# Three of the sixteen double units of a first channel-mix product, made in seven products

## The chip, the cores and the metric

The kernel runs on one core of a Trainium2 chip. The metric is device time in microseconds, the median of several executions. A core has five engines that run side by side, each through its own queue of instructions: TensorE (PE; its weight loads appear as PEld), VectorE (DVE), ScalarE (ACT), GpSimd (POOL) and SyncE (SP). Transfers between main memory and the core's own memory (SBUF) are issued from the queues of SP, ACT and POOL. TensorE writes its results to eight banks of PSUM, from which VectorE and ScalarE evict them.

## The reference, cut to what matters

Two layers (DEPTH = 2) act on x of 512 frames by 1024 features. Each has a mixing part (mLSTM and retention branches with gates), then a channel mix, then a per-layer embedding:

```python
h2 = rmsnorm(x, norm2_g[i])
x = x + jnp.square(jax.nn.relu(h2 @ w_ff1[i] + b_ff1[i])) @ w_ff2[i] + b_ff2[i]
```

`w_ff1` is 1024 by 4096 and `w_ff2` 4096 by 1024. The change concerns the first of these two products, `h2 @ w_ff1`. After it come the per-layer embedding of the layer and, after the second layer, a final norm.

## The kernel before, in words

**Layout and precision.** Activations are kept transposed, features on the 128 partitions and the 512 frames along the free dimension, so x is eight tiles of 128 by 512. Every product is made in split precision: each operand is held as a high part (`wh`, `n2h`, ...; rounded by ScalarE at line 287) and a low part (`wl`, `n2l`, ...; the remainder, by VectorE at line 288), and each product is three matmuls: high by high, high by low, low by high (lines 451 to 453 for whole units, 501 to 503 for units in seven products).

**Whole units.** `t8` (line 442 and on) makes 128 output features: eight input tiles times three matmuls, 24 matmuls over 512 columns into one PSUM bank. Its weights, 128 by 1024 values, come from the array `wstream` with one transfer on SP, and are converted once by ScalarE and once by VectorE.

**Units in seven products.** `run_pair` makes 256 output features at once. The weight block and the activation are cut in two by two quarters, and seven products of quarters or of sums of quarters give the result in place of eight (the scheme of Strassen and Winograd). Each product is 12 matmuls over 256 columns. The order is P1, P5, P6, P2, P3, P7, and the last one, P4, is put off (`later`) until the next unit has made its first 12 matmuls (`flush`). Three PSUM banks serve: P6, P7 and P4 go where P1 was, P3 where P5 was, so each must wait until the earlier one is evicted. Weights come as pieces: A (block B11 and sum t1), C (B22 and t3), B (B21 and the sum t2, formed by VectorE at line 433), D (t4, formed at line 430). t1 and t3 are formed ahead in main memory by transfers on POOL's queue (`step`, line 336: a copy and an adding copy each), in the order of `groups()`, paced by a credit that the matmuls feed. The activation also needs four sums of quarters. For the gates and projections of the mixing part those sums are made once a layer by `xs_sums` through `operand_sums`, and `sevenfold` hands the right quarter to each product; `pair_tiles` evicts the seven products into two 512-column tiles, P1, P5, P6 and P4 by ScalarE and P2, P3 and P7 by VectorE.

**The channel mix.** The 4096 hidden features are four groups of 1024; each group is four double units of 256 (so there are sixteen in a layer), made by `ff1(b, p)` from two whole units. The second product is made group by group in seven products (`ff2`, tiles named o). The order is `ff_order`: f00 to f03, f10, then o00 to o03, f11 to f13, f20, o10 to o13, f21 to f23, f30, o20 to o23, f31 to f33; then, with a half of the embedding product between, o30 to o33. `ff1` evicts each unit by a multiplication with the norm's factor (line 1395, VectorE), Relu and square (lines 1396 and 1397, ScalarE) into a staging buffer `st` (two of them), then forms quarters and sums as operands of the second product (`pair_quarters`, `pair_operand`). The factor of the norm is not known when f00 starts; `n2.finish` and `n2.spread` make it during f00.

**What sets the order.** Weights are loaded and converted ahead in the order of the list of units: `ready` keeps conversion two places ahead for whole units and as `READY` says for pieces; there are three pairs of buffers for converted weights and four for raw ones. The order on each engine is otherwise made by a scheduler that places instructions by priority, which is their place in the program, when their operands and buffers are there.

Of the kernel before, what the change touches and what calls it, by code (L numbers as in the profile page):

```python
# [35 lines left out]
F32 = mybir.dt.float32  # L36
# [6 lines left out]
P = 128  # L43
T = 512
# [34 lines left out]
def ff_order():  # L79

    seq = [("f", 0, p) for p in range(4)]
    for b in range(3):
# [4 lines left out]

PRODUCTS = {"P1": ("A", 0, 0), "P5": ("A", 1, 4), "P2": ("B", 0, 2), "P6": ("B", 1, 5), "P3": ("C", 0, 6),  # L90
            "P7": ("C", 1, 3), "P4": ("D", 0, 1)}

# [35 lines left out]
def groups():  # L128


    g = {}
    for i in range(L):
        def rqk(h):
            return [("w_in", 0, c + k * 256) for k in (h, h + 1) for c in (CRQ, CRK)]

        def rg(h):
            return [("w_in", 0, CRG + h * 512 + 256 * p) for p in range(4)]

        g[i, "rv0"] = [("w_in", 0, CRV)]
        g[i, "rqk0"] = rqk(0)  # L140
        g[i, "gm"] = [("w_in", 0, CGM + 256 * p) for p in (2, 3)]
        g[i, "rg0"] = rg(0)
        g[i, "rv2"] = [("w_in", 0, CRV + 1024)]
        g[i, "rqk2"] = rqk(2)
        g[i, "rg2"] = rg(2)
        g[i, "gr"] = [("w_in", 0, CGR + 256 * p) for p in range(4)]
        for b in range(4):
            g[i, f"ff{b}"] = [("w_ff2", b * 1024, 256 * p) for p in range(4)]
    return g


def unit_list(i):

    u = [("IF",)]

    def t8(w, col, row=0):
        u.append(("T8", w, row, col))

    def v(col):
        for k in range(4):  # L160
            u.append(("V", k, col))

    def pair(g, p):
        u.append(("PAIR", (i, g), p))

    def mqk(h):
        for d in range(2):
            t8("w_in", CQ + h * 256 + d * P)
        for d in range(2):
            t8("w_in", CK + h * 256 + d * P)  # L170

    def mo(h):
        for d in range(2):
            t8("w_in", CO + h * 256 + d * P)

    def rqk(h):
        for a in range(2):
            pair(f"rqk{h // 2 * 2}", h % 2 * 2 + a)

    def rg(h):  # L180
        for a in range(2):
            pair(f"rg{h // 2 * 2}", h % 2 * 2 + a)

    def full(w, col=0, row=0, lo=0, hi=8):
        for c in range(lo, hi):
            t8(w, col + c * P, row)

    mqk(0)
    v(CV)
    full("w_in", CGM, 0, 0, 2)  # L190
    mqk(1)
    mo(0)
    full("w_in", CGM, 0, 2, 3)
    mqk(2)
    mo(1)
    v(CV + 512)
    mqk(3)
    mo(2)
    full("w_in", CGM, 0, 3, 4)
    mo(3)  # L200
    u.append(("WIDE", (i, "rv0"), 0))
    full("w_bm", 0, 0, 0, 4)
    rqk(0)
    for p in (2, 3):
        pair("gm", p - 2)
        full("w_bm", 0, 0, 2 * p, 2 * p + 2)
    rqk(1)
    rg(0)
    u.append(("WIDE", (i, "rv2"), 0))
    rqk(2)  # L210
    rg(1)
    rqk(3)
    full("w_br")
    rg(2)
    rg(3)
    for p in range(4):
        pair("gr", p)
        full("w_br", 0, 1024, 2 * p, 2 * p + 2)
    full("w_out")

    def pairs(seq):
        for kind, b, p in seq:
            if kind == "f":
                t8("w_ff1", b * 1024 + 256 * p)
                t8("w_ff1", b * 1024 + 256 * p + P)
            else:
                pair(f"ff{b}", p)

    pairs(ff_order()[0])
    u.append(("PE", 0))  # L230
    pairs(ff_order()[1])
    u.append(("PE", 1))
    full("w_pe_gate")
    return u


def build(ctx, tc, ins, out):
# [8 lines left out]
    def phase(name, side, bufs=1):  # L246
        return tc.alloc_tile_pool(name=name, bufs=bufs, side=side, reuse_waits="tile")
# [478 lines left out]
    def bcol(i, n, k):  # L726
        o, _ = _B[n]
        return bc[:, i, o + k:o + k + 1]
# [210 lines left out]
    for i in range(L):  # L939
# [443 lines left out]
        shift(cur["ff"], ph_side, True)  # L1383
        cur["ntmp"] = 2
        hid = {}

        def ff1(b, p):

            nm = f"l{i}f{b}{p}"
            hid[b, p] = [cur["ff"].tile([P, 7 * S], F32R, name=f"l{i}h{a}{b}{p}", tag=f"h{a}", bufs=5) for a in "hl"]  # L1390
            st = cur["ff"].tile([P, 8 * S], F32, name=nm + "st", tag="st", bufs=2)

            def evac(d, o):
                a = st[:, d * T:(d + 1) * T]
                ve.tensor_tensor(a, o, n2.b, OP.mult)
                ac.activation(a, a, AF.Relu, bias=bcol(i, "bf1", 8 * b + 2 * p + d))
                ac.activation(a, a, AF.Square)

            o = t8(n2.act, f"{nm}0")
            if b == 0 and p == 0:  # L1400
                n2.finish()
                o1 = t8(n2.act, f"{nm}1")
                n2.spread()
                evac(0, o)
                evac(1, o1)
            else:
                evac(0, o)
                evac(1, t8(n2.act, f"{nm}1"))
            pair_quarters(st, *hid[b, p])
            pair_operand(nm, st, *hid[b, p])  # L1410
# [39 lines left out]
        for kind, b, p in first:  # L1450
# [3 lines left out]
            if (b, p) == (3, 1):  # L1454
                pth, ptl = [cur["ff"].tile([P, 2, T], F32R, name=f"l{i}pt{a}", tag=f"h{a}", bufs=5) for a in "hl"]
                for k in range(2):
                    t = tmp(f"l{i}ptr{k}")
                    nc.scalar.dma_start(t, ins["pT"][i, k])
                    split(t, pth[:, k, :], ptl[:, k, :])
            ff1(b, p)  # L1460
        n2_pool.release()
        n3_pool = phase(f"n3{i}", act_side)
        n3 = Norm(f"l{i}n3", i, "g3", acts(n3_pool, f"l{i}n3"))
# [235 lines left out]
```

## Time and profile before

| | |
|---|---|
| median of 3 runs | 2336.89 us (2335.52 to 2338.47) |
| the profiled execution | 2338.24 us, span 2336.5 us |
| PE busy | 2317.7 us, 99% |
| DVE busy | 1722.3 us, 74% |
| ACT busy | 1224.1 us, 52% |
| POOL busy | 401.4 us, 17% |
| moved by DMA | 394.95 MB, mean 169 GB/s |

The span is the stretch from the first to the last instruction of one profiled execution; the time of that execution holds a little around it. Busy times are sums over an engine's instructions. Matmuls overlap in TensorE's pipeline, so the time from one matmul's start to the next tells more than the length of one. Layers are named l0 and l1; in the first layer the channel mix's first product runs from 772.6 us to about 1068 us.

### The profile page before, as it was taken

The page shows a single profiled execution, that of the slowest core. Times are in us where ns is not written, and L with a number is a line of the kernel's source. Part 1 is how long each engine was busy: PE and PEld are TensorE (multiplying, and loading weights), DVE is VectorE, ACT ScalarE, POOL GpSimd, SP SyncE. Part 2 cuts the span into 40 slices and gives each one's busy share as a digit, 9 for nine tenths or more (in the row PEclk, how much of TensorE's full clock was granted, in tenths as well). Part 3 has the DMA queues.
Part 4 walks back from the last instruction along what each step waited for, and adds up shares of the span by engine and source line. Part 5 has one row for each costly group of instructions (what it writes and reads, how often), then busy time and mean ns, then how long its engine had stood idle before and what let it go on. Part 6 is the DMA issues. An engine that isn't in the chain of part 4 may idle for free.

```text
span 2336.5 us, 35728 instructions
## 1 busy us (share of the span) xinstructions
PE 2317.7 (99%) x13664; PEld 2055.3 (88%) x13664; DVE 1722.3 (74%) x2658; ACT 1224.1 (52%) x1771; POOL 401.4 (17%) x618
## 2 busy tenths in 40 slices
PE   9999999999999999999999999999999999999998
PEld 8888898898998898899888888998989988998997
DVE  7878767896665577678778777778957656776785
ACT  6756544554554445445557564454636445445464
POOL 3122212112114212112422221000000020000012
PEclk9999999999999999999999999999999999999999
DMA  6665886668688777777766666434443442333431
GB/s 214 166 172 155 249 230 183 195 176 224 176 239 253 197 205 191 206 203 189 212 177 172 154 178 196 145 121 151 129 138 114 157 154 99 127 109 94 136 122 55
DMA packets 150540, 394.95 MB, mean 169 GB/s; under 512 B 19344, under 2 KB 22800, under 8 KB 150368
## 3 DMA queue, kind: packets, MB, share of 16 engines
q1 hardware_dynamic: 99808, 247.50, 32.6%
q0 software_dynamic: 35152, 117.73, 22.9%
q10 hardware_dynamic: 15408, 27.43, 3.5%
q8 instruction: 107, 1.75, 0.3%
q14 instruction: 65, 0.53, 0.1%
HBM read 373.71 MB, written 123.73 MB: 213 GB/s over the span
## 4 chain that ended last, share of the span: by engine, by line
PE 84%; issue 6%; DVE 5%; DMA 2%; ACT 2%; POOL 1%; SPq 0%; ACTq 0%; DVEq 0%; POOLq 0%
PE l1f L451 2%; PE l0f L451 2%; PE l0f L452 2%; PE l1f L452 2%; PE l1f L453 2%; PE l0f L453 2%; PE l1br L451 1%; PE l0br L451 1%; PE l0br L453 1%; PE l1br L452 1%; PE l0br L452 1%; PE l1br L453 1%; PE l0pg L451 1%; PE l0pg L453 1%; PE l1bm L451 1%
## 5 line engine op out<-in xcount | busy, mean ns | idle before, releaser
L287 ACT ACTIVATE wh<-wr 128x1024 fp32r<-128x1024 f32 (+1 forms) x223 | 231.2, 1044 | 286.4 <-issue 62.9
L288 DVE TENSOR_TENSOR wl<-wr,wh 128x1024 fp32r<-128x1024 f32 (+1 forms) x221 | 272.4, 1234 | 73.7 <-ACT wh L287 73.5
L287 ACT ACTIVATE wh_B<-wr 128x1024 fp32r<-128x1024 f32 x100 | 105.9, 1059 | 149.8 <-PE l1bm L452 13.1
L288 DVE TENSOR_TENSOR wl_B<-wr,wh_B 128x1024 fp32r<-128x1024 f32 x100 | 122.0, 1220 | 20.8 <-ACT wh_B L287 20.8
L287 ACT ACTIVATE wh_C<-wr 128x1024 fp32r<-128x1024 f32 x76 | 80.3, 1057 | 64.4 <-issue 9.6
L287 ACT ACTIVATE wh_D<-wr 128x512 fp32r<-128x512 f32 x76 | 48.0, 631 | 124.8 <-DVE wr L433 57.2
L288 DVE TENSOR_TENSOR wl_A<-wr,wh_A 128x1024 fp32r<-128x1024 f32 x76 | 92.8, 1221 | 20.2 <-ACT wh_A L287 20.2
L288 DVE TENSOR_TENSOR wl_C<-wr,wh_C 128x1024 fp32r<-128x1024 f32 x76 | 94.3, 1241 | 16.1 <-ACT wh_C L287 15.7
L287 ACT ACTIVATE wh_A<-wr 128x1024 fp32r<-128x1024 f32 x76 | 80.0, 1052 | 47.2 <-PE l0f L452 6.7
L451 PE MATMUL l1f<-l1n2h,wh 128*128 128x512 f32 x256 | 99.9, 390 | 0.0
L451 PE MATMUL l0f<-l0n2h,wh 128*128 128x512 f32 x256 | 99.8, 390 | 0.0
L453 PE MATMUL l0f<-l0n2h,wl 128*128 128x512 f32 x256 | 99.7, 389 | 0.0
L453 PE MATMUL l1f<-l1n2h,wl 128*128 128x512 f32 x256 | 99.7, 389 | 0.0
L452 PE MATMUL l0f<-l0n2l,wh 128*128 128x512 f32 x256 | 99.6, 389 | 0.0
L452 PE MATMUL l1f<-l1n2l,wh 128*128 128x512 f32 x256 | 99.6, 389 | 0.0
L288 DVE TENSOR_TENSOR wl_D<-wr,wh_D 128x512 fp32r<-128x512 f32 x76 | 52.5, 690 | 36.9 <-ACT wh_D L287 35.8
L662 POOL TENSOR_TENSOR l1n3sum<-l1n3sum,l1n3sq 128x512 f32<-128x512 f32 x6 | 9.2, 1539 | 330.8 <-ACT l1n3sum L654 309.8
L430 DVE TENSOR_TENSOR wr<-wr,wr 128x512 f32<-128x512 f32 x76 | 52.2, 687 | 16.2 <-DMA wr<-wpairs 15.3
L453 PEld LDWEIGHTS l1f<-l1n2h,wl 128*128 128x128 f32 x256 | 48.0, 188 | 10.1
L453 PEld LDWEIGHTS l0f<-l0n2h,wl 128*128 128x128 f32 x256 | 48.0, 188 | 10.0
L452 PEld LDWEIGHTS l0f<-l0n2l,wh 128*128 128x128 f32 x256 | 48.1, 188 | 9.9
L452 PEld LDWEIGHTS l1f<-l1n2l,wh 128*128 128x128 f32 x256 | 48.1, 188 | 9.8
(5626 smaller groups left out, 8558.3 us busy)
## 6 DMA issues: line engine op xcount, KB each, us to landing
wr<-wstream SPq DMA_DIRECT2D x219, 512.0 KB, 4.5
wr<-wpairs SPq DMA_DIRECT2D x228, 256.0 KB, 3.0
wr<-wwide SPq DMA_DIRECT2D x24, 512.0 KB, 3.7
s0t<-wwide POOLq DMA_DIRECT2D x10, 512.0 KB, 5.6
s4t<-wwide POOLq DMA_DIRECT2D x10, 512.0 KB, 6.4
s12t<-wwide POOLq DMA_DIRECT2D x10, 512.0 KB, 5.4
s16t<-wwide POOLq DMA_DIRECT2D x10, 512.0 KB, 5.5
s1t<-wpairs POOLq DMA_DIRECT2D x16, 256.0 KB, 4.1
```

The lines of the kernel that those rows point to most:

```text
L287: a = ac.activation(hi_ap, src, AF.Copy)
L288: return a, ve.tensor_sub(lo_ap, src, hi_ap.bitcast(F32))
L430: ve.tensor_tensor(raws[n, "B"][:, Q:], kept.pop((n, "A"))[:, Q:], r[:, :Q], OP.add)
L451: te.matmul(o, sh, mh, start=first, stop=False)
L452: te.matmul(o, sh, ml, start=False, stop=False)
L453: cur["mm"] = te.matmul(o, sl, mh, start=False, stop=last)
L662: (add or gp).tensor_tensor(self.sum, self.sum, sq, OP.add)
```

## The change

Per layer, the double units f12, f22 and f32 (`FPAIRS`: group b = 1, 2, 3, each with p = 2) are made as units in seven products. Their weights leave `wstream` and become groups `fp1`, `fp2` and `fp3` of one unit each, whose sums t1 and t3 are formed in main memory like the others', just ahead of those of `ff1`, `ff2` and `ff3`. The activation, the normed x, needs its sums of quarters: `n2_sums(k)`, k = 0 to 3, makes them after each of f00 to f03, using the staging buffers `st` and a new pool of tiles (`nsh`, `nsl`; in the last layer `nsh` lies in the tiles of `big`). The two results are put together in the first two 512-column parts of `st` by `pair_tiles`, with the second one's sign turned, and the multiplication, Relu (with `scale=sign`), square and operand follow from there when P4 is done.

```diff
+FPAIRS = ((1, 2), (2, 2), (3, 2))
...
         for b in range(4):
+            f = [p for c, p in FPAIRS if c == b]
+            if f:
+                g[i, f"fp{b}"] = [("w_ff1", 0, b * 1024 + 256 * p) for p in f]
             g[i, f"ff{b}"] = [("w_ff2", b * 1024, 256 * p) for p in range(4)]
...
-            if kind == "f":
+            if (b, p) in FPAIRS and kind == "f":
+                pair(f"fp{b}", [q for c, q in FPAIRS if c == b].index(p))
+            elif kind == "f":
...
+        ns_pool = phase(f"ns{i}", act_side)
+        if i == L - 1:
+            ns = [a.bitcast(F32R) for a in big(f"l{i}nsh", F32)]
+        else:
+            ns = [ns_pool.tile([P, T], F32R, name=f"l{i}nsh{k}", tag="nh", bufs=KT) for k in range(KT)]
+        ns = ns, [ns_pool.tile([P, T], F32R, name=f"l{i}nsl{k}", tag="nl", bufs=KT) for k in range(KT)]
+        n2_seven = sevenfold(n2.act, ns)
+
+        def n2_sums(k):
+            st = cur["ff"].tile([P, 8 * S], F32, name=f"l{i}ns{k}", tag="st", bufs=2)
+            v = [st[:, a * T:(a + 1) * T] for a in range(4)]
+            for a in range(2):
+                ve.tensor_tensor(v[a], *[t[2 * k + a].bitcast(F32) for t in n2.act], OP.add)
+            operand_sums(f"l{i}ns{k}", v[:2], *[t[2 * k:2 * k + 2] for t in ns], v[2:])
...
-            def evac(d, o):
+            def evac(d, o, sign=1.0):
                 a = st[:, d * T:(d + 1) * T]
                 ve.tensor_tensor(a, o, n2.b, OP.mult)
-                ac.activation(a, a, AF.Relu, bias=bcol(i, "bf1", 8 * b + 2 * p + d))
+                ac.activation(a, a, AF.Relu, bias=bcol(i, "bf1", 8 * b + 2 * p + d), scale=sign)
                 ac.activation(a, a, AF.Square)
 
+            if (b, p) in FPAIRS:
+                def consume(y):
+                    for d in range(2):
+                        evac(d, y[d], SIGN[d])
+                    pair_quarters(st, *hid[b, p])
+                    pair_operand(nm, st, *hid[b, p])
+
+                pair_tiles(nm, n2_seven, consume, [st[:, d * T:(d + 1) * T] for d in range(2)])
+                return
...
             ff1(b, p)
+            if b == 0:
+                n2_sums(p)
+        ns_pool.release()
```

`operand_sums`, which is called and not changed, forms the four sums of quarters with four instructions of VectorE over 256 columns, and then splits each of two 512-column tiles into its high and low part.

## The prediction

> **What bounds the kernel now.** I read the head of the page first, then the chain that ended last, then the waits of TensorE, and last the busy times by stretch, because the change touches only the channel mix.
>
> ```profile
> span 2336.5 us, 35728 instructions
> PE 2317.7 (99%) x13664; PEld 2055.3 (88%) x13664; DVE 1722.3 (74%) x2658; ACT 1224.1 (52%) x1771; POOL 401.4 (17%) x618
> PE 84%; issue 6%; DVE 5%; DMA 2%; ACT 2%; POOL 1%; SPq 0%; ACTq 0%; DVEq 0%; POOLq 0%
> PE l0r0o0c L501 <- ACT l0r0o0y L571: 2.0, 1, 2.0
> ...
> PE l1o30a L503 <- DVE wl_B L288: 0.3, 1, 0.3
> PE l0o30a L503 <- DVE wl_B L288: 0.3, 1, 0.3
> ```
>
> TensorE is busy 99% of the span and makes 84% of the chain. Its waits are small: the longest is 2.0 us, and in the channel mix the largest is 0.3 us, where the second product block (o30) waits for VectorE to finish the low half of weight piece B. So time can be won only by giving TensorE less to do, and lost only by making another engine late. VectorE, at 74%, is the one that could become late. The stretches (columns after the microseconds: PE, PEld, DVE, ACT, POOL, each with its instructions, then the granted clock, DMA share, GB/s) show where:
>
> ```profile
> 776.50:787.00 10.50, 10.50 (x51) 8.78 (x50) 4.46 (x12) 2.60 (x3) 3.42 (x3) 1.00 0.55 164
> 787.00:828.90 41.90, 41.90 (x187) 34.71 (x186) 29.42 (x39) 25.93 (x34) 5.81 (x8) 1.00 0.80 193
> 828.90:846.00 17.10, 17.02 (x143) 16.80 (x143) 16.53 (x27) 10.14 (x12) 3.13 (x5) 1.00 0.66 192
> 874.50:907.10 32.60, 32.60 (x145) 27.01 (x144) 21.21 (x28) 18.93 (x24) 8.14 (x12) 1.00 0.77 179
> 654.00:716.70 62.70, 62.70 (x398) 56.91 (x397) 41.87 (x58) 30.82 (x43) 16.52 (x25) 1.00 0.89 243
> ```
>
> The first two rows are the first group of layer 0 (f00 to f10), the third is the start of the second product's block o0, where VectorE has 0.6 us free in 17.1. The fourth holds f11 to f13, the place of a new unit. The fifth is the gate stage, which already alternates one unit of seven products with two whole units. The granted clock is 1.00 in all.
>
> **The change, part by part.**
>
> *TensorE's work.* A double unit of the first product is two whole units of 24 matmuls over 512 columns. Its pitch is read from the evictions of f12 and f13. The price of a unit in seven products (84 matmuls over 256 columns) between whole units is read from the gate stage, whose evictions repeat every (unit in seven products + two whole units):
>
> ```profile
> 885.33 0.69 DVE L1395 TENSOR_TENSOR l0f12st<-l0f,l0n2rb 128x512 f32<-128x512 f32 x1 [0.94 <-PE l0f L453]
> 896.21 0.69 DVE L1395 TENSOR_TENSOR l0f13st<-l0f,l0n2rb 128x512 f32<-128x512 f32 x1 [0.35 <-PE l0f L453]
> ...
> 661.34 0.69 DVE L1352 TENSOR_TENSOR l0brl<-l0br,l0brl 128x512 f32<-128x512 f32 x1 [4.25 <-PE l0br L453]
> 724.08 0.69 DVE L1352 TENSOR_TENSOR l0brl<-l0br,l0brl 128x512 f32<-128x512 f32 x1 [4.74 <-PE l0br L453]
> ```
>
> Two whole units take 896.21 - 885.33 = 10.88 us. The gate stage takes (724.08 - 661.34) / 3 = 20.91 us a period, so its unit in seven products costs 20.91 - 10.88 = 10.03 us. A replaced double unit saves 0.85 us; there are three in each of two layers: -5.1 us. The expected eighth of 10.88, 1.36, is not reached because the short matmuls run somewhat over half the long ones' time:
>
> ```profile
> 913.75 0.28 PE L501 MATMUL l0o10c<-l0hh,wh_A 128*128 128x256 f32 x1
> 915.16 0.29 PE L501 MATMUL l0o10a<-l0hh,wh_B 128*128 128x256 f32 x1
> ...
> 1081.71 0.28 PE L501 MATMUL l0o30a<-l0hh,wh_C 128*128 128x256 f32 x1
> 1083.07 0.28 PE L501 MATMUL l0o31a<-l0hh,wh_A 128*128 128x256 f32 x1
> ```
>
> Twelve of them take 1.41 us, 0.1175 us each, against 10.88 / 48 = 0.2267 for a long one. In one stretch they took 1.36 us (0.1133 each); I take the gate stage's price, since that has the new units' neighbours, and keep the other pace for the range. [...]
>
> *Weights of a new unit.* VectorE and ScalarE convert 3.5 tiles of 1024 columns in place of 2, and VectorE forms two sums:
>
> ```profile
> L288 DVE TENSOR_TENSOR wl<-wr,wh 128x1024 fp32r<-128x1024 f32 (+1 forms) x221 | 272.4, 1234 | 73.7 <-ACT wh L287 73.5
> L288 DVE TENSOR_TENSOR wl_B<-wr,wh_B 128x1024 fp32r<-128x1024 f32 x100 | 122.0, 1220 | 20.8 <-ACT wh_B L287 20.8
> L288 DVE TENSOR_TENSOR wl_D<-wr,wh_D 128x512 fp32r<-128x512 f32 x76 | 52.5, 690 | 36.9 <-ACT wh_D L287 35.8
> L430 DVE TENSOR_TENSOR wr<-wr,wr 128x512 f32<-128x512 f32 x76 | 52.2, 687 | 16.2 <-DMA wr<-wpairs 15.3
> L573 DVE TENSOR_TENSOR l0gr1y<-l0gr1b,l0gr1y x1: 420/420/420, 672.6 to 672.6; 128x256 f32<-128x256 f32 x1
> ```
>
> That is 3 x 1.22 + 0.69 + 2 x 0.69 = 5.7 us against 2 x 1.23 = 2.5. Three of the seven products are evicted by VectorE (3 x 0.42 = 1.3), four by ScalarE; the two multiplications by the norm stay, now reading SBUF. VectorE gains 3.2 + 1.3 = 4.5 us a unit: in f11 to f13 it goes from 21.2 of 32.6 to 25.7 of 31.8 us, 81%, and still has 6 us free. I cost this at nothing; it is the load under which the gate stage runs without loss (41.87 of 62.70 is lower, 67%, so this is a bound and not a copy). ScalarE had 18.93 of 32.6 and has room.
>
> *Order.* Product 7 of a new unit is put off past the first 12 matmuls of f(b,3), and only then come the multiplication, Relu, square and operand. Block o(b) needs them; between lie the rest of f(b,3) and f(b+1,0) (for b = 3 the first half of the embedding product), at least 10.88 us, against some 21.21 / 3 = 7.1 us of VectorE's work for a double unit. Covered. If VectorE were behind, the first matmuls of o(b,0) would stand.
>
> *Sums of the normed x.* Four sets a layer, all issued in the first group:
>
> ```profile
> L1159 DVE TENSOR_TENSOR l0xsr<-l0xnh,l0xnl 128x512 f32<-128x512 f32 x8 | 5.2, 685 | 0.0
> L600 DVE TENSOR_TENSOR l0xs0u<-l0xsr x1: 418/418/418, 145.1 to 145.1; 128x256 f32<-128x256 f32 x1
> L288 DVE TENSOR_TENSOR l0xsl<-l0xs0u,l0xsh x2: 683/683/683, 148.2 to 150.1; 128x512 fp32r<-128x512 f32 x2
> ```
>
> A set is 2 x 0.685 + 4 x 0.418 + 2 x 0.683 = 4.4 us on VectorE, 17.6 us a layer. VectorE's free time is 6.0 us in 776.5 to 787 (while TensorE makes f00 and the norm's factor is not there yet) and 12.5 in 787 to 828.9: 18.5 us. So it just fits, with 0.9 us over, if the first set is moved ahead of the norm's factor. The sets also take turns with the units in the two staging buffers (st), so f01 to f03 can no longer overlap there; their first evictions come a little later, and free PSUM banks carry that. Weights of whole units are converted a unit ahead and can take delays. What cannot is this:
>
> ```profile
> 828.69 1.06 ACT L287 ACTIVATE wh_B<-wr 128x1024 fp32r<-128x1024 f32 x1 [2.83 <-PE l0f L452]
> 829.79 1.22 DVE L288 TENSOR_TENSOR wl_B<-wr,wh_B 128x1024 fp32r<-128x1024 f32 x1 [0.18 <-ACT wh_B L287]
> 831.55 0.35 PE L501 MATMUL l0o00a<-l0hh,wh_B 128*128 128x256 f32 x1
> ```
>
> Piece B of o00 is ready at 831.01 and used at 831.55; what VectorE still owes at 829 goes straight to TensorE, and the next 17 us have 0.6 us free. The charge lies between 0 (all fits) and 17.6 - 12.5 = 5.1 us a layer less the 0.2 us or so of slack here, 4.9 (nothing moved ahead of 787). Because the sum says it fits with 0.9 over, I take one wait like o30's, 0.3 to 0.4 us a layer: +0.8 us.
>
> *DMA and queues.* Each new unit loads five blocks of 256 KB for two of 512 KB (SP), and its sums of weight blocks are four more DMAs on POOL, 24 in all, paced by matmuls.
>
> ```profile
> L336 POOL DMA_DIRECT2D s9t<-wpairs x16: 501/652/1145, 603.2 to 667.2; - x16
> L387 SPq DMA_DIRECT2D wr<-s9t x8: 423/436/673, 882.4 to 930.1; - x8
> ```
>
> Sixteen steps take 64 us and are done 215 us before use, so 12 more a layer put the later ones back by some 51 us and no load waits. No wait of TensorE in this trace names a DMA. I cost it at nothing.
>
> The sum: -5.1 + 0.8 = -4.3 us. The profiled execution took 2338.24 us (span 2336.5), which would become 2333.9; the median of the runs is 2336.89, 1.35 lower, so I predict 2332.6.
>
> **The rivals.** A measurement of this kernel tells about 0.2%, 4.7 us, from no change; the bounds are 2332.2 and 2341.6.
>
> 1. *Everything hides, or the products run at their faster pace.* Without the +0.8 the time is 2331.8. At 1.36 us a product, a new unit takes 7 x 1.36 + 0.16 (what the gate stage's 10.03 has over 7 x 1.41) = 9.68, saving 6 x 1.20 = 7.2 us: 2329.7. For it: 1081 us. Against: the gate stage never shows it.
> 2. *Each new unit pays for its entry.* Piece B is there as late as in o00, and VectorE carries 4.5 us more. Six waits of 0.3 us give 2332.6 + 1.8 = 2334.4; one 1 us each, 2338.6. For it: the waits of o30. Against: none at the gate stage's entries.
> 3. *Slower: VectorE's debt in the first group.* Where the sets cannot use the time before 787 us, 4.9 us a layer reach TensorE at o00 and o01: -5.1 + 9.8 = +4.7, 2341.6; each further microsecond a layer adds 2. It decides for slower from 4.9 us of debt at 829. For it: 97% busy in 828.9 to 846. Against: the 18.5 us.
> 4. *The short matmuls give nothing*, at 0.1295 us or more each (10.88 / 84): 2336.9 + 0.8 = 2337.7. The gate stage excludes it almost wholly.
>
> **How the numbers follow.** The forecast, 2331.5 to 2333.8, 0.44, lies across the bound: 0.20 faster, 0.24 within. Rival 1: 0.16, faster. Rival 2: 0.18, within. Rival 4: 0.02, within. Rival 3: 0.20, slower. So faster 0.36, within 0.44, slower 0.20. The range of 8 in 10 reaches from 2330.0, just short of the faster pace, to 2341.5, the onset of rival 3, leaving out some 0.04 below and 0.16 above.
>
> **What would show it.** In the changed profile the evictions around f12 should stand 10.0 us apart where they were 10.9; TensorE should show no wait above 0.4 us at fb2 units; VectorE should be near 97% busy from 776 to 829 us and the wait for wl_B at o00 should stay under 0.5 us. A start of o00's block more than 1 us behind the sum, waits of o00 or o01 on VectorE, or evictions of f12 more than 10.3 us apart would make the prediction wrong.

## The result and the profile after

The changed kernel takes 2344.34 us in the median of 12 runs (2341.0 to 2348.42), the kernel before 2338.69 us in 12 runs beside it (2335.52 to 2341.36). The ratio is 1.0023, with a 95% interval of 1.0015 to 1.003: slower by some 5 us, where 2332.6 us was predicted. On another occasion (e9 below) it was 2342.91 against 2338.44, 1.0019 (1.001 to 1.0028). Line numbers in the changed kernel stand 8 higher in the helpers (L430 is now L438, L501 is L509). One thing about the kernel before has to be put right: the sum that VectorE makes of the raw pieces A and C (t2) is line 430 and the sum that gives piece D (t4) is line 433; the description above has them the other way round.

The head of the changed kernel's page:

```profile
span 2341.5 us, 36426 instructions
PE 2317.6 (99%) x13880; PEld 2063.7 (88%) x13880; DVE 1768.5 (76%) x2764; ACT 1246.3 (53%) x1823; POOL 413.4 (18%) x642
```

Some of its longest waits of TensorE (engine, tile, line, what it waited for: us in all, times, longest), those of layer 0's channel mix first:

```profile
PE l0o00a L509 <- DVE l0x L1455: 1.3, 1, 1.3
PE l0o20a L509 <- DVE l0x L1455: 0.9, 1, 0.9
PE l0o23a L509 <- DVE l0x L1455: 0.6, 1, 0.6
...
PE l0r0o0c L509 <- ACT l0r0o0y L579: 2.3, 1, 2.3
PE l0r2o1a L509 <- DVE l0r2o1y L587: 1.6, 1, 1.6
PE l1r0brqa L509 <- DVE l1r0brqy L587: 0.9, 1, 0.9
```

TensorE is busy 2317.6 us against 2317.7 before, though it was given less to do; five of these six stand at places that had 0.7 us or less before. To see where the time goes, I split both traces at instructions that both have. First starts of TensorE's products, kernel before and changed kernel (start, duration, line, product):

```profile
778.31 0.28 PE L669 MATMUL l0n2ss<-ones_r,l0n2sum 128*128 128x2 f32 x2
828.72 0.28 PE L501 MATMUL l0o00a<-l0hh,wh_A 128*128 128x256 f32 x1
857.44 0.28 PE L501 MATMUL l0o03a<-l0hh,wh_A 128*128 128x256 f32 x1
912.33 0.28 PE L501 MATMUL l0o10a<-l0hh,wh_A 128*128 128x256 f32 x1
1125.19 0.28 PE L669 MATMUL l0n3ss<-ones_r,l0n3sum 128*128 128x2 f32 x2
1935.00 0.28 PE L669 MATMUL l1n2ss<-ones_r,l1n2sum 128*128 128x2 f32 x2
2282.14 0.28 PE L669 MATMUL l1n3ss<-ones_r,l1n3sum 128*128 128x2 f32 x2
```

```profile
782.07 0.28 PE L677 MATMUL l0n2ss<-ones_r,l0n2sum 128*128 128x2 f32 x2
832.48 0.28 PE L509 MATMUL l0o00a<-l0hh,wh_A 128*128 128x256 f32 x1
863.08 0.28 PE L509 MATMUL l0o03a<-l0hh,wh_A 128*128 128x256 f32 x1
917.21 0.28 PE L509 MATMUL l0o10a<-l0hh,wh_A 128*128 128x256 f32 x1
1131.12 0.28 PE L677 MATMUL l0n3ss<-ones_r,l0n3sum 128*128 128x2 f32 x2
1941.76 0.28 PE L677 MATMUL l1n2ss<-ones_r,l1n2sum 128*128 128x2 f32 x2
2287.62 0.28 PE L677 MATMUL l1n3ss<-ones_r,l1n3sum 128*128 128x2 f32 x2
```

The differences give the stages. Two further profiles of the changed kernel (e9, e18) and one of the kernel before (e17) stand beside them:

| stage, us | before | e17, before | after | e9, after | e18, after | mean difference |
|---|---|---|---|---|---|---|
| first product to layer 0's mix | 777.26 | 777.57 | 781.02 | 781.77 | 778.73 | +3.1 |
| channel mix, layer 0 | 346.88 | 346.79 | 349.05 | 349.47 | 349.46 | +2.5 |
| between the mixes | 809.81 | 808.54 | 810.64 | 811.13 | 810.84 | +1.7 |
| channel mix, layer 1 | 347.14 | 346.85 | 345.86 | 344.40 | 346.02 | -1.6 |

So the gain is there in one mix of two, and two thirds of what is lost (3.1 and 1.7 of 7.3 us) lie outside the mixes, in code that the change does not touch. Three profiles against two are few for those two stages; how far they scatter over all 20 profiles is told behind the last experiment. The parts:

*The units.* From o03 to o10, with f12 between, it is 917.21 - 863.08 = 54.13 us against 912.33 - 857.44 = 54.89: a new unit saves 0.76 us. Where nothing else comes in, as in all of layer 1's later groups, every new unit does so: -2.3 us a layer.

*The sums of the normed x.* From o00 to o03 it is 30.60 against 28.72 us in layer 0 (+1.9), and 29.65 against 28.67 in layer 1 (+1.0). Busy times by stretch (columns as in the prediction) of the changed kernel, shifted by the 3.8 us that it is behind:

```profile
780.30:790.80 10.50, 10.50 (x52) 8.76 (x51) 4.51 (x12) 2.60 (x3) 4.28 (x5) 1.00 0.71 188
790.80:832.70 41.90, 41.90 (x187) 34.73 (x186) 41.81 (x69) 28.24 (x40) 6.97 (x10) 1.00 0.70 183
832.70:849.80 17.10, 15.37 (x128) 14.82 (x127) 15.78 (x26) 9.56 (x13) 1.35 (x2) 1.00 0.75 209
```

VectorE's 4.51 us in the first row are what it had before (4.46): no set was moved ahead of the norm's factor. All four stand behind it, VectorE has no gap left in 41.9 us, and o00 pays.

*Late loads.* The instruction that adds raw A and raw C, in the channel mix of layer 0, kernel before (L430) and changed kernel (L438, with what VectorE sat idle for ahead of it):

```profile
L430 DVE TENSOR_TENSOR wr<-wr,wr x16: 681/688/693, 809.3 to 1094.7; 128x512 f32<-128x512 f32 x16
```

```profile
L438 DVE TENSOR_TENSOR wr<-wr,wr x19: 676/685/695, 832.5 to 1100.6; 128x512 f32<-128x512 f32 x19
...
  DMA wr<-wpairs: 12.1, 4
```

Before, none of the 16 waited for a load. Now four of the 19 wait 12.1 us together. What stands behind the waiting instruction is seen in VectorE's own order (the bracket is the idle time ahead of it and what ended it):

```profile
1037.73 0.41 DVE L1455 TENSOR_TENSOR l0x<-l0x,l0o23b 128x256 f32<-128x256 f32 x1
1041.26 0.69 DVE L438 TENSOR_TENSOR wr<-wr,wr 128x512 f32<-128x512 f32 x1 [3.12 <-DMA wr<-wpairs]
1041.87 0.41 DVE L1455 TENSOR_TENSOR l0x<-l0x,l0o23c 128x256 f32<-128x256 f32 x1
```

This is the sum for f32, a new unit. Its raw C has not landed. The evictions of o23's P3 (in the rows above) and P7 (at 1043.34 us) come behind it, though the last matmuls of those products started at 1038.76 and 1040.17, before the sum; TensorE waits 0.6 us for the bank of P7. The same sum for o20 waits 3.94 us at 984.27. Together they cost 2.2 us in this profile (o20's stage 30.10 in place of 28.73, and 49.62 where 48.77 was due from o23 to o30).

*Between the mixes.* GpSimd's steps that form the sums of weights are 376 in place of 352. Their last one, and VectorE's sum of A and C at the start of layer 1's projections, in order of time, kernel before and changed kernel:

```profile
1411.65 0.86 POOL L336 DMA_DIRECT2D s23t<-wpairs  x1 [2.21 <-PE l1r0vc L547]
...
1471.66 0.69 DVE L430 TENSOR_TENSOR wr<-wr,wr 128x512 f32<-128x512 f32 x1 [0.68 <-DMA wr<-wpairs]
```

```profile
1480.62 0.69 DVE L438 TENSOR_TENSOR wr<-wr,wr 128x512 f32<-128x512 f32 x1 [3.37 <-issue]
...
1494.17 0.78 POOL L344 DMA_DIRECT2D s29t<-wpairs  x1 [0.56 <-DVE l1r0brqu L1094]
```

The stretch between the two ends (columns as above; the DMA share is the last but one), kernel before and changed kernel:

```profile
1412.00:1495.00 83.00, 83.00 (x482) 72.95 (x482) 62.61 (x82) 35.53 (x49) 2.79 (x5) 1.00 0.52 166
```

```profile
1412.00:1495.00 83.00, 82.08 (x456) 71.33 (x454) 59.64 (x78) 33.98 (x44) 25.38 (x38) 1.00 0.89 245
```

The steps end 83 us later, the DMA engines are 89% busy in place of 52%, and the sum of A and C stops VectorE for 3.37 us (4.68 in e18) in place of 0.68. The view names no releaser for this stop ("issue"), but the trace has the load: one half of raw C was issued at 1475.19 us and landed at 1480.54, just ahead of the sum, after 5.35 us; in the kernel before it took 2.62 us, from 1468.92 to 1471.54. TensorE waits at l1r0brqa, 0.9 us here and 2.2 in e18, for an eviction behind the sum. In the kernel before that wait is not in the list.

*The clock.* In two of the three profiles the stretch ahead of layer 0's mix holds something else. TensorE by stretch (busy, granted clock, DMA share, GB/s), kernel before and changed kernel, at r0o0:

```profile
406.00:408.00 2.00, 2.00 (x17) 1.00 0.04 14
408.00:410.00 2.00, 2.00 (x19) 1.00 0.00 0
410.00:415.00 5.00, 5.00 (x39) 1.00 0.33 105
```

```profile
406.00:408.00 2.00, 0.21 (x1) 1.00 0.59 176
408.00:410.00 2.00, 2.00 (x16) 0.84 0.01 2
410.00:415.00 5.00, 5.00 (x32) 0.72 0.00 0
```

And two of the products in it:

```profile
409.48 0.41 PE L510 MATMUL l0r0o0a<-l0xsl,wh_B 128*128 128x256 f32 x1
...
412.47 0.41 PE L510 MATMUL l0r0o0c<-l0xsl,wh_C 128*128 128x256 f32 x1
```

After the wait of 2.3 us the granted clock falls, and from 409.48 to 412.47 us there are 14 steps of short products, 0.214 us each in place of 0.118; the whole stretch costs 1.4 us. The three profiles of the changed kernel have this at r0o0 twice, the two of the kernel before not at all.

### The profile page after: what moved, and what is told of

Read it like the earlier page. It is cut to its first block, busy times and chain, and to the rows that moved or that the text cites. A ratio compares the mean times of both kernels' runs of the same rounds, so it can differ in the third digit from the quotient of the medians.

```text
span 2341.5 us, 36426 instructions
## 1 busy us (share of the span) xinstructions
PE 2317.6 (99%) x13880; PEld 2063.7 (88%) x13880; DVE 1768.5 (76%) x2764; ACT 1246.3 (53%) x1823; POOL 413.4 (18%) x642
## 5 line engine op out<-in xcount | busy, mean ns | idle before, releaser
L295 ACT ACTIVATE wh<-wr 128x1024 fp32r<-128x1024 f32 (+1 forms) x211 | 218.6, 1043 | 218.6 <-issue 67.1
L296 DVE TENSOR_TENSOR wl<-wr,wh 128x1024 fp32r<-128x1024 f32 (+1 forms) x209 | 257.4, 1233 | 63.2 <-ACT wh L295 58.5
L438 DVE TENSOR_TENSOR wr<-wr,wr 128x512 f32<-128x512 f32 x82 | 56.3, 687 | 43.4 <-DMA wr<-wpairs 37.5
L459 PE MATMUL l0f<-l0n2h,wh 128*128 128x512 f32 x208 | 81.2, 391 | 0.0
L459 PE MATMUL l1f<-l1n2h,wh 128*128 128x512 f32 x208 | 81.2, 391 | 0.0
L460 PE MATMUL l1f<-l1n2l,wh 128*128 128x512 f32 x208 | 81.0, 389 | 0.0
L461 PE MATMUL l1f<-l1n2h,wl 128*128 128x512 f32 x208 | 81.0, 389 | 0.0
L461 PE MATMUL l0f<-l0n2h,wl 128*128 128x512 f32 x208 | 81.0, 389 | 0.0
L460 PE MATMUL l0f<-l0n2l,wh 128*128 128x512 f32 x208 | 81.0, 389 | 0.0
L441 DVE TENSOR_TENSOR wr<-wr 128x512 f32<-128x512 f32 x82 | 56.2, 686 | 0.8
L461 PEld LDWEIGHTS l0f<-l0n2h,wl 128*128 128x128 f32 x208 | 39.0, 188 | 8.4
```

The lines of the kernel that those rows point to most:

```text
L295: a = ac.activation(hi_ap, src, AF.Copy)
L296: return a, ve.tensor_sub(lo_ap, src, hi_ap.bitcast(F32))
L438: ve.tensor_tensor(raws[n, "B"][:, Q:], kept.pop((n, "A"))[:, Q:], r[:, :Q], OP.add)
L441: ve.tensor_tensor(r[:, :Q], r[:, :Q], r[:, Q:], OP.add)
L459: te.matmul(o, sh, mh, start=first, stop=False)
L460: te.matmul(o, sh, ml, start=False, stop=False)
```

## The experiments

The first theory: the mixes lose by the sums' debt and by late loads that stop VectorE's queue, and the rest is scatter. The rivals: the new layout of the weights in main memory costs by itself; or the new units do not save what the mix shows. Fifteen other kernels and three repeats were run. Medians of the kernel before on the same occasions were 2338.77, 2338.77, 2338.44 and 2338.73 us.

**e1, the layout alone:** the kernel before, its weights in main memory laid out with the blocks of the three units as pieces.

```
+            f = [p for c, p in FPAIRS if c == b]
+            if f:
+                g[i, f"fp{b}"] = [("w_ff1", 0, b * 1024 + 256 * p) for p in f]
```

> The kernel before with the weight blocks of the three units placed in the array of weight blocks as in the changed kernel, and room for their sums in main memory, but nothing of it used: every engine's instructions are those of before. The changed kernel's profile is 3.8 us behind before reaching the channel mix of layer 0, where all instruction orders are still the same. Theory A (VectorE's debt in the first group explains the loss, the 3.8 us are chance of one execution): 2338.7 +- 1.5, no change. Theory B (the placement of data in main memory makes transfers of the mixing part late): +3 to +5 us, 2342 to 2344, and the channel mix of layer 0 starts 3 to 4 us later than 778 us.

**e2, the sums alone:** the changed kernel with `FPAIRS = ()`, so that the sums are made and not used.

> The sums of the normed x are made as in the changed kernel, but no unit uses them: all sixteen double units are whole. Theory A: VectorE is busy without a gap from about 787 to 846 us and TensorE waits in blocks o00 and o01; the two channel mixes together lose 3 us (1.9 + 1.0 read from the changed kernel), 2341.7. If the debt explained all of the 10.7 us between the -5.1 forecast for the units and the +5.6 measured, it would be +10 us, 2349. Theory B: at most +3 as well, since the placement is that of before.

**e3, the units alone:** the sums of the normed x are left out, and the new units multiply by the normed x in their place.

```
-        n2_seven = sevenfold(n2.act, ns)
+        n2_seven = sevenfold(n2.act, n2.act)
```

> The six units in seven products as in the changed kernel, but the sums of the normed x are not made: the products that should read them read the normed x's tiles instead, so this part of the computation is left out and the output is another. Theory A: 6 x -0.8 = -4.6 to -5.1 us, 2334. Theory B: the placement's +4 stays, so 2338 to 2339, with the mixing part of layer 0 as late as in the changed kernel. A third cause, transfers late in the blocks o20 and o23 of layer 0 (the changed kernel lost 2.6 us there), would show as waits there with the first group undisturbed.

**e4, the sums early:** the additions go to ScalarE, which reads x and not the normed x, and two of the four sets stand ahead of f00.

```
-                ve.tensor_tensor(v[a], *[t[2 * k + a].bitcast(F32) for t in n2.act], OP.add)
+                ac.activation(v[a], x[2 * k + a], AF.Copy, scale=n2.col(2 * k + a))
...
+            if (b, p) == (0, 0):
+                n2_sums(0)
+                n2_sums(1)
             ff1(b, p)
-            if b == 0:
+            if b == 0 and p > 1:
                 n2_sums(p)
```

> The changed kernel with the two additions of each set made by ScalarE from x (a scaled copy) instead of by VectorE from the high and low parts, and the first two sets issued ahead of f00. VectorE is relieved of 4 x 1.4 = 5.5 us in the first group and may use its 6 us free before the norm's factor. Theory A: no wait above 0.5 us in o00 and o01, the channel mixes gain 2.3 to 2.5 us each, 2334 to 2335. Theory B: 3 us better than the changed kernel, 2341, no faster than before.

Measured:

| kernel | median, us | ratio to before (95%) | mix, layer 0 | mix, layer 1 | o00 to o03, layer 0 |
|---|---|---|---|---|---|
| e1, layout | 2340.58 | 1.0005 (0.9996 to 1.0014) | 347.27 | 346.03 | 28.71 |
| e2, sums | 2341.61 | 1.0011 (1.0003 to 1.002) | 348.80 | 348.10 | 30.26 |
| e3, units | 2339.46 | 1.0003 (0.9994 to 1.0011) | 347.66 | 344.92 | 28.72 |
| e4, sums early | 2339.81 | 1.0003 (0.9994 to 1.0012) | 350.05 | 344.95 | 28.66 |

The layout alone shows no loss that can be told from none. The sums alone cost 1.5 us in layer 0's first group and 1.0 in layer 1's (29.64 there), and e4 takes both away between o00 and o03 (28.66 and 28.65): the debt is the sums' work in VectorE's queue behind the norm's factor. (e4 moves two sets and takes the additions from VectorE at once; which of the two does it was not tried. In layer 0 it pays elsewhere: from the norm to o00 it is 51.28 us in place of 50.41.) By the medians, e2 lies 2.8 us above the kernel before on its occasion and e3 0.7, 3.5 together, where the changed kernel lies 4.5 to 5.7 above; the rest is not covered by these two runs. The units alone save 2.2 us in layer 1's mix, as three times 0.76 says, but layer 0's mix grows by 0.8: there e3 waits at o20 and o23 like the changed kernel, and e4 even longer. That set the next question.

**e5 to e8, the sum of A and C behind the conversion of C.** In the channel mix of both layers an order is put on VectorE's queue, for the second product's units; the new units, f32 among them, are left as they are. e5 is e3 with it, e6 is e4, e7 the changed kernel, e8 the kernel before.

```
-            ve.tensor_tensor(raws[n, "B"][:, Q:], kept.pop((n, "A"))[:, Q:], r[:, :Q], OP.add)
+            t = ve.tensor_tensor(raws[n, "B"][:, Q:], kept.pop((n, "A"))[:, Q:], r[:, :Q], OP.add)
+            if units[n][1][1][:2] == "ff":
+                tc.add_manual_dep(t.ins, cur["prep"][1].ins.name, ORDER, reason="order of the sum")
```

> The changed kernel without the sums of the normed x (the new units multiply by other data), and in the channel mix the sum of a second-product unit's raw pieces A and C, which waits for the load of C, is ordered in VectorE's queue behind the conversion of C, so that nothing waits behind it that C's own conversion would not hold up. Theory (in layer 0 this sum stands at the head of VectorE's queue before its load has landed, 3.75 and 3.98 us in the run without the order, and stops the evictions behind it): layer 0's mix falls from 347.66 to about 344.7 us (346.88 in the kernel before, less three units of 0.76), the stage from the first product of o20 to that of o23 from 29.90 to 28.73, layer 1's mix stays at 344.9; time 2 to 3 us under that run. Rival (it is the late load itself that TensorE lacks, as the weights of o20): layer 0's mix stays within 0.5 us of 347.66.

> The kernel with the sums made by ScalarE from x ahead of the norm's factor, and with the sum of A and C ordered behind the conversion of C as in the run without sums. Theory: both losses are gone. Layer 0's mix 345 to 346 us (350.05 without the order), layer 1's 345; the two together 3 to 4 us under the kernel before, and the time 0 to 4 us under it, by what the layout does to the mixing stages. Rival (the load is late for TensorE itself): layer 0's mix above 349 us, time 1 us over the kernel before.

> The changed kernel as it was given, with the one order of the sum of A and C. Theory: the debt of the sums in the first group stays (30.6 and 29.65 us from the first product of o00 to that of o03, 28.7 in the kernel before), the late load's loss in layer 0 goes: mix of layer 0 from 349.05 to between 346 and 347 us. The mixing of layer 0, which has the same instructions in the same order as the changed kernel's, took 535.45 us there and 532.7 in the kernel before: if the placement of the added weight sums made this, it comes again at 535; if it was this one execution, it is 532 to 533.5. Rival on the load: mix of layer 0 within 0.5 us of 349.05.

> The kernel before with the one order of the sum of A and C in the channel mix. Theory: its loads land in time, so there is nothing to gain: both mixes within 0.3 us of 346.88 and 347.14, the same time within 1 us. Rival (the order by itself is worth time, whatever the units): both mixes 0.5 us or more shorter.

All four became slower: 2347.46, 2348.54, 2347.6 and 2347.79 us; ratios 1.0034 (1.0022 to 1.0046), 1.0043 (1.0031 to 1.0056), 1.0044 (1.0027 to 1.006) and 1.0041 (1.0027 to 1.0055). The control e8 says why: the order has a price of its own. The mixes of e8 take 352.51 and 349.83 us, 5.6 and 2.7 more than before, with waits of this kind in units that follow each other without anything between (waits of TensorE in layer 0's mix, e8):

```profile
PE l0o32a L501 <- DVE l0x L1424: 0.9, 1, 0.9
...
PE l0o33a L501 <- DVE l0x L1424: 0.8, 1, 0.8
PE l0o32a L503 <- DVE wl_B L288: 0.5, 1, 0.5
```

So the early place of that sum is worth time where loads are in time: it lets piece B be converted early. In layer 0's mix ScalarE's conversion of B waits for the sum seven times in e8, 17.2 us in all, and once, 2.3 us, in the kernel before. The edit was too wide to test the theory, and left out the sum of f32 that the theory is about; my expectation for e8 (no change) was wrong. The mixes of e5 (352.01, 348.10), e6 (351.97, 348.08) and e7 (353.31, 348.52) prove nothing on the loads.

**e10 and e11, the order on two units only.** As before, but for f32 and o20 of layer 0 alone; e10 is e3 with it, e11 is e4. **e9** is the changed kernel once more, **e12** is e4 with units and sums in layer 1 alone.

```
+            if units[n][1:] in (((0, "fp3"), 0), ((0, "ff2"), 0)): tc.add_manual_dep(t.ins, ...)
...
-            if (b, p) in FPAIRS and kind == "f":
+            if (b, p) in FPAIRS and kind == "f" and i == L - 1:
```

> The changed kernel once more, unchanged. Its two mixes took 0.89 us more than those of the kernel before in the profiled execution, but its median lies 5.65 us above, and the stages ahead of the channel mix of layer 0, whose instructions and order are those of the kernel before, took 3.76 us more. Theory A (those stages scatter from one execution to the next): layer 0 from its mixing's start to the second norm, 535.45 us there, comes nearer to 532.7, and the time falls to between 1 and 3 us over the kernel before. Theory B (the changed program itself makes these stages longer, by where its data or its instructions lie): 535 us and 5 to 6 us over it again. The mixes 349.05 and 345.86 us within 0.3 in both.

> The changed kernel without the sums of the normed x, with only two of the sums of raw A and C, those of f32 and o20 in layer 0, ordered behind the conversion of C; all others stand where the run without sums has them. Theory (these two, waiting 3.75 and 3.98 us for their loads, stop VectorE's queue): layer 0's mix falls from 347.66 to 344.6 to 345.2 us; the stage from o20's first product to o23's from 29.90 to 28.73, that from o23's to o30's from 50.48 to 48.8. In the runs with the order on all units that order had a price of its own: 5.6 us in layer 0's mix and 2.7 in layer 1's for the kernel before. Rival (the load of C itself comes too late for TensorE): layer 0's mix stays above 347 us.

> The kernel with the sums made by ScalarE ahead of the norm's factor, and the same two orders. Theory: layer 0's mix falls from 350.05 to about 346 us (344.6 and 0.87 for the first unit's later start), layer 1's stays at 344.95; the mixes together 3 us under the kernel before, the time 0 to 3 us under it. Rival (late loads bind TensorE): layer 0's mix above 348.5 us, time over the kernel before.

> The three units and their sums of the normed x (made by ScalarE) in layer 1 alone; layer 0's channel mix is that of the kernel before. Theory (layer 0 loses by loads that land late while GpSimd's queue forms sums of weights, layer 1 has no such transfers): layer 0's mix 346.9 us, layer 1's 344.95 against 347.14; time 2 us under the kernel before if nothing else moves. Rival (the change's gain is lost outside the mixes whatever the layer): mixes as said, time the same as or over the kernel before.

e9: 2342.91 us, 1.0019 (1.001 to 1.0028), nearer to theory B. e10: 2338.83, 1.0006 (0.9996 to 1.0015). e11: 2340.53, 1.0015 (1.0005 to 1.0025). e12: 2337.72, 0.9997 (0.9988 to 1.0006). For f32 the theory holds: from o23 to o30 it is 48.77 and 48.76 us in e10 and e11, the full 0.76 under the kernel before, where e3 and e4 have 50.48 and 50.34. For o20 it falls: its stage became longer, 31.75 and 33.14 against 29.90 and 32.41. The waits of e10 around it:

```profile
PE l0o20a L509 <- DVE l0x L1442: 1.6, 1, 1.6
PE l0o20b L511 <- DVE wl_B L296: 1.3, 1, 1.3
```

Moved behind the conversion, the sum delays piece B (wl_B) there, so for o20 the rival is right: the load itself is late for TensorE. Layer 0's mix is 346.57 us in e10 and 350.41 in e11, above what the theory gave for both. e12, without new units in layer 0, has no late load there and saves in layer 1's mix, but its median is 0.7 us under the kernel before, not clear of no change, where 2 us was expected. Its mix of 342.40 us is lower than three units explain, because 480 of some 1,200 short products there ran at the quicker of the two paces that the prediction shows (0.1133 us against 0.1178). Counted in every profile, this pace comes in both kernels, 0 to 480 of some 1,200 products a mix, 208 and 152 in e17, the kernel before: it is no part of the change.

**e13, one raw buffer more:** e3 with a fifth raw buffer in layer 0's channel mix. **e14 to e16, the wait at r0o0:** ScalarE's conversion of a reloaded value tile, which waits for its load, is ordered behind the eviction of r0o0's P5 in both layers; e14 is the kernel before with it, e15 the changed kernel, e16 is e12.

```
+        if i == 0:
+            cur["room"] = range(at["unit"] + 8, units.index(("PAIR", (i, "ff3"), 0)))
...
+                c, _ = split(lo[:, :T].bitcast(F32), hi[:, :T], lo[:, :T])
+                if behind and j == NT - 1:
+                    tc.add_manual_dep(c.ins, behind.ins.name, ORDER, reason="order of the conversion")
```

> The changed kernel without the sums of the normed x, and with one raw buffer more for the pieces of layer 0's channel mix (a fifth, in the pool of the channel mix); no order is changed by hand. Theory (the three pieces that a new unit holds of the four raw buffers make the next unit's loads start late): the waits of 3.75 and 3.98 us at the sums of raw A and C in layer 0 fall under 1 us, layer 0's mix falls from 347.66 us to between 344.6 and 345.2 at the slower pace of the short products. Rival (the loads are slow whenever they start, because GpSimd's transfers of the weight sums run beside them): the waits stay above 2.5 us and the mix above 346.5.

> The kernel before, with one edit in the mixing part of both layers: ScalarE's conversion of the fourth reloaded value tile, which waits for its load, is ordered behind the eviction of r0o0's third product, for which TensorE waits (2.0 us in layer 0, 1.7 in layer 1). In the changed kernel this wait was 2.3 us, and the 33 products after it ran at 0.213 us instead of 0.118, at a granted clock of 0.84 and 0.72 in two windows of 2 and 5 us: 1.43 us more. Theory (waits of over 2 us at this place, and the slow stretch that sometimes follows, are the scatter that the medians show): both waits fall by a microsecond or more, no slow stretch follows, and the time falls by 2 to 5 us. Rival (the wait only moves to the next step): time within 1 us of the kernel before.

> The changed kernel with the same edit at r0o0. Theory (of the 4.5 to 5.7 us that its median lies above the kernel before, the mixes explain 1 to 2, and a wait at r0o0 followed by a slow stretch of TensorE most of the rest): its distance to the kernel before with the same edit falls to between 1 and 2.5 us, and the mixing of layer 0, 535.45 and 536.18 us in the two profiles, comes to 531 to 533. Rival (the rest has nothing to do with this wait): it stays 4 us or more above the kernel before with the same edit.

> The three units and their sums in layer 1 alone, with the same edit at r0o0 in both layers. Theory: the two gains add, 2 us from layer 1's mix and 2 to 5 us from the edit; time 4 to 7 us under the kernel before. Rival (the edit at r0o0 gives nothing): 0 to 2 us under it.

The 33 products of these texts are a miscount; the trace shows the 14 steps told above.

e13 took 2337.56 us, 0.9998 (0.9989 to 1.0008). VectorE's waits for loads at that sum, e3 (960 to 1060 us) and e13 (the whole mix of layer 0):

```profile
DVE wr L438 <- DMA wr<-wpairs: 7.7, 2, 4.0
```

```profile
DVE wr L438 <- DMA wr<-wpairs: 2.4, 1, 2.4
```

Over the whole mix e3 has four such waits, 10.1 us. The wait at o20 is gone, and its stage is 28.73 us like the kernel before. So for o20 the number of raw buffers makes the load late: a new unit holds three of the four (A kept, C, and B, which becomes D). The wait at f32 fell from 3.98 to 2.43 only and still delays o23; the mix is 346.73 us, short of the theory's 345.2. There the rival has a part: the load of raw C was issued 5.9 us earlier than in e3 (1025.04 in place of 1030.90), but the sum could start only 4.2 us earlier (1032.70 in place of 1036.87). What is left is a slow transfer, 7.66 us from its issue to the sum, where the changed kernel's page has 3.5 us in the median from issue to landing for loads of these pieces; what slows it was not tried.

e14: 2338.06 us, 1.0005 (0.9994 to 1.0015). e15: 2343.23, 1.002 (1.0011 to 1.0028). e16: 2335.28, 0.9988 (0.9979 to 0.9997). Waits of TensorE in e14, and TensorE by stretch at r0o0 of layer 1:

```profile
PE l1r0o0c L501 <- ACT l1r0o0y L571: 2.5, 1, 2.5
PE l0r0o0c L501 <- ACT l0r0o0y L571: 1.2, 1, 1.2
```

```profile
1560.00:1562.00 2.00, 0.18 (x2) 1.00 0.08 25
1562.00:1566.00 4.00, 3.27 (x16) 0.63 0.00 0
```

In layer 0 the wait fell from 2.0 to 1.2; in layer 1 it did not, and the clock fell to 0.63 after it. The edit by itself can't be told from no change. In e15 both waits at r0o0 are under 1 us, and its first stage takes 777.82 us, as before; but its median stays 5.2 us above that of e14. So the rival is right: this wait is not where the rest of the loss comes from. In the profile of e15 the loss stands elsewhere. TensorE by stretch at o23 in e15:

```profile
1040.00:1042.00 2.00, 0.09 (x1) 1.00 1.02 199
1042.00:1044.00 2.00, 2.00 (x13) 0.69 0.63 197
1044.00:1046.00 2.00, 2.00 (x6) 0.50 0.82 234
1046.00:1050.00 4.00, 4.00 (x19) 0.98 0.27 69
```

Here it is the late load of f32 that stops TensorE, and the granted clock falls to 0.50 after it: 52.49 us from o23 to o30, mix 351.49. e16 is the one kernel whose interval lies below the kernel before, by some 3 us: new units where their loads are in time and their sums have a place. How much of it is the edit at r0o0 is not known: e12, without it, and e14, without the units, are each not clear of no change.

**e17 and e18, both kernels once more,** for the table of stages.

> The kernel before once more, unchanged, for a second profile of it: the one that all stages are compared with may be a lucky execution. Theory A (the stages outside the channel mixes scatter from execution to execution): its way from the first instruction of TensorE to the second norm of layer 0 takes 1 to 3 us more than the 777.26 us of the first profile, or the stages between the two mixes do, at the same order of instructions. Theory B: 777 and 810 us within 0.5, and what the changed kernel takes more there belongs to the change.

> The changed kernel a third time, beside it. Theory A: to the second norm of layer 0 it takes anything from 777 to 782 us. Theory B: 781 to 782 us, as in the first two profiles (781.02 and 781.77). In both: layer 0's mix 349 us or, where the clock falls after the wait at o23, 350.5 to 351.5; layer 1's mix 344.4 to 345.9.

They took 2336.57 and 2342.0 us. Neither theory holds whole: the first stage of the changed kernel was 778.73 (so it does scatter), but all three profiles of it are above both of the kernel before.

All 20 profiles together say more of the two stages outside the mixes. The way to layer 0's mix takes 776.89 to 778.73 us in the 14 profiles whose granted clock stays at 1.00 there, and 779.99 to 781.77 in the six that have a slow stretch at r0o0 or r2o1: two of the changed kernel, e6, e7, e11, and also e8, whose instructions up to that mix are those of the kernel before. So the fall of the clock parts the profiles, and it can come without the change; whether the change makes it more frequent, these few profiles can't say. The stage between the mixes takes 809.59 to 811.61 us in the 12 profiles of kernels with 376 steps and 808.54 to 811.61 in the other eight (352 steps, or 364), 0.4 us less on the mean. The wait at l1r0brqa is in all of the 12 (0.4 to 2.6 us) and in none of the eight; but the wait at l1r0o0 behind it is 0.7 to 1.6 us in the 12 and 1.6 to 2.5 in the eight, so most of what the one adds the other saves, and the +1.7 of the table is mostly scatter.

## Why the prediction was wrong

*TensorE's work: right, a little too large.* A new unit was priced at 10.03 us and saves 0.76 in place of 0.85, so it costs 10.12; six save 4.6, not 5.1. The short pace, 0.1133 us a product, had no part in it.

*Weights of a new unit, and order: right.* No wait of TensorE falls on the new units f12, f22 and f32 themselves, and o10 waits 0.2 us.

*Sums of the normed x: the step that failed first.* The 18.5 us of free time counted 6.0 us ahead of the norm's factor on a condition, "if the first set is moved". It was not moved: its place in the program is behind f00. The charge is +1.9 and +1.0 us in place of twice 0.4, and e2, with the sums alone, lies 2.8 us above the kernel before. The sign that the prediction named for this is there: TensorE waits for VectorE at o00 and o01, 1.3 and 0.4 us. That is rival 3's mechanism at less than its 4.9 us a layer; that other work of VectorE could slip is my reading and was not tried. (By the prediction's own rows, 831.01 and 831.55, the slack at o00 was 0.5 us and not 0.2, so its bound would have been 4.6.)

*DMA and queues: the second step that failed, and by as much.* "I cost it at nothing" rested on no wait of TensorE naming a DMA. In these traces TensorE's list names only the last link: its 0.6 us at o23 are put down to VectorE, and the 3.12 us that VectorE's sum waited for its load ahead of that stand in VectorE's rows alone. The new units hold three of four raw buffers, and 24 steps more keep GpSimd's transfers going 83 us longer, where "put the later ones back by some 51 us and no load waits" stood. That figure holds for twelve steps (in e12, with twelve more, the last one is at 1462.5 us, 51 us later, and nothing waits at l1r0brqa), but the steps of both layers stand in one queue, and ahead of layer 1's mixing all 24 have been added. The first costs 2.2 us in layer 0, and more with the clock's fall (52.49 us from o23 to o30 in e15, 49.62 in the first profile of the changed kernel). The second comes with 0.9, 2.6 and 2.2 us at l1r0brqa in the three profiles, of which the shorter wait at l1r0o0 (1.2, 0.9 and 1.4 us against 1.7 and 2.0) gives a part back; no run changed the number of steps alone.

*The remainder.* +3.1 us ahead of layer 0's mix on the mean of three profiles. A third is the slow stretch at r0o0 in two of them (1.4 and 1.6 us); r2o1, whose wait is 1.6 us against 0.7 and 0.5 in the kernel before, gives another microsecond; there too the sum of A and C waits for its load (1.95 us, and 1.80 in e18, against 0.86 and 0.92 in the kernel before), with as much moved beside it as before (12.05 MB from 560 to 620 us in e18, 12.10 in e17). Why that load lands later is open. The layout in main memory does not give the 3.1 us by itself: e1 is not clear of zero, and e3, e5, e10 and e13, with the changed kernel's layout and its 376 steps, take 777.18 to 778.61 us to layer 0's mix. What makes the clock fall there in one execution and not in the next stays open too.

## What to carry to other kernels

Before an instruction that waits for a load is given an early place on an engine, ask what stands behind it: here a sum that waited 3.12 us for its load held up two evictions, and TensorE's list named VectorE, not the load. Count the buffers that a new unit holds and for how long, not only its bytes, and follow added background transfers to their new end. Free time of an engine counts only if the work is really placed in it; an order by hand must be as narrow as the wait that it removes, since an early place that wins elsewhere is lost with it (e8).

## What the runs showed of the hardware

A wait of about 2 us can cost more than its length: at r0o0 in the changed kernel TensorE waited 2.3 us, and the slow stretch behind the wait cost 1.4 us more. In all 20 profiles, 28 stops of TensorE lasted 2.0 us or longer (gap between starts less the product's own pace); after 13 of them the products ran at about half pace (0.214 us in place of 0.118 in the changed kernel), for some 3.4 us in e15 (twice the 0.31 x 2 + 0.50 x 2 + 0.02 x 4 us that its rows lack) and as long in the changed kernel (twice 0.16 x 2 + 0.28 x 5), and 1.1 to 1.6 us were lost where most of that was short products; of some 65 stops of 1 to 2 us (those at the start and the end of the kernel left out) only two did, both at one place where they follow each other. The length was no criterion: 2.04 us did it in e9, 2.64 did not in e18.
